# Per-head sums of squares of queries and keys: one full-precision product replaced by two single-rate products on a high/low split

## The chip, the cores and the metric

The kernel runs on one core of a Trainium2 chip. The metric is the device time of one execution in microseconds (us). The core has TensorE (PE, products), VectorE (DVE), ScalarE (ACT), GpSimd (POOL) and SyncE (SP, whose queue issues nearly all DMAs). Every engine and the SP queue work through their own instructions in order.

## The reference, cut to what matters

One layer of a decoder trunk, for 2048 prompt tokens and 8 sample tokens of width 1024:

```python
h = rmsnorm(x)*(1+scale1)+shift1
u, q, k, v, a_pool, a_attn = split(h @ w_in)
q = rope(rmsnorm(q.reshape(..., N_HEADS, HEAD_DIM), q_norm_g), pos)
k = rope(rmsnorm(k.reshape(..., N_HEADS, HEAD_DIM), k_norm_g), pos)
x += g1*(sig(a_pool)*(PoolMix(u) @ w_pool_br) + sig(a_attn)*(DilatedAttn(q,k,v) @ w_attn_br)) @ w_out
x += g2*relu(h2 @ w_up)**2 @ w_down
```

12 heads of 64 stand in 3 groups of 4 (g = 2, 1, 0). `rmsnorm` of a query or key divides each head by the root of the mean of its 64 squares. That sum of squares is what the change is about. Queries and keys are also outputs (the key windows) and the operands of the attention.

## The kernel before, in words

**Products.** Activations lie transposed, channels on the partitions. Each dense product with a weight is made of three products at the single rate on operands split into a high and a low part of type float32r (`mm3`, which calls `mm`, L153, for every product): high by high, high by low, low by high. A weight block (`load_w`, L178 to L186) comes by an SP DMA into a raw tile `wr` (3 buffers), ACT casts the high part (L183), POOL subtracts for the low part (L184), the pair being the tile `wh` (3 buffers). One block is loaded ahead.

**Stages.** Tokens go in two chunks. In the first one (1032 tokens, in pieces of 512, 256 and 264 columns) the projections for queries, keys and values run nearly alone, about 80 to 291 us. In the second chunk (1024 tokens, pieces of 512) they run from 742 to 1130 us, laced with the attention of groups that are ready (scores `ps_s`, transposes `ps_t`, outputs `ps_o`). After that come the gates, the output projection and the feed-forward products, which take most of the 3 ms.

**One query or key piece.** `qk_out` empties the two product tiles of a piece with ACT: a scaled copy `ab` (L381) and the squares `qsq` (L382). `after_qk` (L390 to L446) then runs 30 times: 18 with 512 columns (6 of them in the first chunk), 6 with 256 and 6 with 264. Each time it loads the rotary table `cs` (L395, SP), POOL adds the two square tiles (L396), POOL and DVE make the rotation (tiles `rt` and `ro`, L400 to L405), PE multiplies the added squares by a block of ones, which sums over the 32 partitions of each head and leaves the sum on all of them (`ps_hs`, a product in float32), ACT takes the root (L410), DVE the reciprocal (L411) and the two scalings (L413), ACT and POOL split the result into high and low (`ohl`, L423 and L424), and SP stores it to `qst` or `kst` (L426, L429) and for late keys to an output (L433). Later SP loads the attention's `slab` tiles from `qst` and `kst`. In the second chunk there is one `cs`, one `ohl`, two `qsq` and two product tiles in PSUM.

**What sets the order.** PE's order is written by hand: `Order` keeps an emulated clock which every product advances by a given duration, and the body of `after_qk` is a coroutine that comes back `HS_AT` (6500 ns of that clock) after it began, at the next poll, to put its `ps_hs` between other products. Attention batches are coroutines of the same kind. The other engines' order is made by a scheduler; instructions under `first()` get a higher priority.

**Start.** `opening` (first products while the conditioning is worked out) takes its raw weight tiles from the same 3 `wr` buffers. Constants, the block of ones `hones` among them, come in one DMA, the tile `cp` (L226).

## Time and profile before

| | before |
|---|---|
| runs, median (lowest to highest) of 3 | 3072.97 us (3070.19 to 3075.37) |
| the profiled execution, its own time | 3068.15 us |
| its span in the trace | 3066.3 us |
| mean granted clock of TensorE | 0.982 |
| busy: PE, DVE, ACT, POOL | 96%, 52%, 32%, 31% |
| PE products of `ps_hs` | 30 instructions, 60 records in the trace (two passes each) |

In a profile, the busy time of an engine is what its instructions took; the time an engine sat idle is put down to whatever ended the wait. A product's record covers more than its own step, since products are pipelined: its cost is read from the chain of waits, which follows PE from start to start.

### The profile page before, as it was taken

The page shows a single profiled execution, that of the slowest core. Times are in us where ns is not written, and L with a number is a line of the kernel's source. Part 1 is how long each engine was busy: PE and PEld are TensorE (multiplying, and loading weights), DVE is VectorE, ACT ScalarE, POOL GpSimd, SP SyncE. Part 2 cuts the span into 40 slices and gives each one's busy share as a digit, 9 for nine tenths or more (in the row PEclk, how much of TensorE's full clock was granted, in tenths as well). Part 3 has the DMA queues.
Part 4 walks back from the last instruction along what each step waited for, and adds up shares of the span by engine and source line. Part 5 has one row for each costly group of instructions (what it writes and reads, how often), then busy time and mean ns, then how long its engine had stood idle before and what let it go on. Part 6 is the DMA issues. An engine that isn't in the chain of part 4 may idle for free.

```text
span 3066.3 us, 40880 instructions
## 1 busy us (share of the span) xinstructions
PE 2956.4 (96%) x16220; PEld 2526.4 (82%) x16220; DVE 1590.4 (52%) x2645; ACT 970.6 (32%) x1765; POOL 960.6 (31%) x504
## 2 busy tenths in 40 slices
PE   7999999999898799999999999999999999999999
PEld 3899788887787688887899999999877788888887
DVE  5656442542744524447865555545578554444444
ACT  4333332434544434433521221221235212111211
POOL 2565341433433311224531222122245312221221
PEclk9999999999899889999999999999999999999999
DMA  6544752335777878876221111111272211111111
GB/s 239 176 139 156 275 174 91 129 107 151 198 191 209 186 191 217 235 233 236 94 96 35 56 49 46 45 49 49 84 250 83 76 42 56 48 49 42 55 43 68
DMA packets 204431, 379.09 MB, mean 124 GB/s; under 512 B 43232, under 2 KB 99904, under 8 KB 203456
## 3 DMA queue, kind: packets, MB, share of 16 engines
q1 hardware_dynamic: 192720, 359.63, 38.2%
q10 hardware_dynamic: 11520, 16.85, 1.5%
q8 instruction: 128, 2.10, 0.3%
q14 instruction: 63, 0.52, 0.1%
HBM read 294.89 MB, written 81.75 MB: 123 GB/s over the span
## 4 chain that ended last, share of the span: by engine, by line
PE 77%; DMA 6%; DVE 5%; issue 3%; ACT 2%; POOL 2%; SPq 1%; DVEq 0%; ACTq 0%; POOLq 0%
PE ps_dn L153 22%; PE ps_up L153 22%; PE ps_g L153 9%; PE ps_qk L153 5%; PE ps_v L153 4%; PE ps_wo L153 4%; PE ps_u L153 3%; PE ps_s L153 2%; PE ps_o L153 1%; PE ps_pb L153 1%; POOL wh L184 1%; PE ps_ada L153 1%; PE ps_ab L153 1%; DMA t1d<-ta 1%; DMA cs<-in_rope 1%
## 5 line engine op out<-in xcount | busy, mean ns | idle before, releaser
L184 POOL TENSOR_TENSOR wh<-wr,wh 128x1024 fp32r<-128x1024 f32 (+1 forms) x274 | 650.1, 2380 | 1679.0 <-ACT wh L183 1607.5
L153 PE MATMUL ps_dn<-rt,wh 128*128 128x512 f32 (+2 forms) x3840 | 726.2, 350 | 6.4 <-POOL wh L184 3.3
L153 PEld LDWEIGHTS ps_dn<-rt,wh 128*128 128x128 f32 x3840 | 618.9, 188 | 109.2 <-POOL wh L184 4.2
L183 ACT CAST wh<-wr 128x1024 fp32r<-128x1024 f32 (+1 forms) x306 | 309.4, 1023 | 730.7 <-issue 562.3
L1274 DVE SCALAR_TENSOR_TENSOR xa<-ps_dn,mod,xa 128x512 f32<-128x512 f32 (+1 forms) x640 | 405.2, 641 | 202.8 <-PE ps_dn L153 201.0
L153 PE MATMUL ps_g<-h,wh 128*128 128x512 f32 (+2 forms) x1920 | 390.5, 355 | 0.4 <-POOL wh L184 0.4
L153 PE MATMUL ps_up<-hb,wh 128*128 128x264 f32 (+2 forms) x2304 | 371.5, 320 | 0.0
L153 PE MATMUL ps_up<-ha,wh 128*128 128x512 f32 x1536 | 365.7, 394 | 0.0
L153 PEld LDWEIGHTS ps_up<-hb,wh 128*128 128x128 f32 x2304 | 332.3, 188 | 36.0
L153 PEld LDWEIGHTS ps_g<-h,wh 128*128 128x128 f32 x1920 | 309.4, 191 | 48.4 <-POOL wh L184 0.9
L153 PEld LDWEIGHTS ps_up<-ha,wh 128*128 128x128 f32 x1536 | 287.1, 188 | 64.2 <-issue 0.5
L153 PE MATMUL ps_qk<-h,wh 128*128 128x512 f32 (+2 forms) x1440 | 301.1, 363 | 8.9 <-POOL h L318 6.5
L1258 DVE TENSOR_TENSOR r<-r 128x512 f32<-128x512 f32 (+2 forms) x160 | 99.3, 620 | 387.0 <-ACT r L1257 386.9
L153 PEld LDWEIGHTS ps_qk<-h,wh 128*128 128x128 f32 x1440 | 235.9, 194 | 50.8 <-POOL h L318 7.5
L1260 DVE TENSOR_TENSOR rt<-r,rt 128x512 fp32r<-128x512 f32 (+2 forms) x160 | 217.8, 1361 | 81.8 <-ACT rt L1259 81.7
L1257 ACT ACTIVATE r<-ps_up 128x512 f32<-128x512 f32 (+2 forms) x160 | 82.1, 513 | 415.0 <-PE ps_up L153 415.0
L153 PE MATMUL ps_v<-wh,h 128*128 128x256 f32 (+1 forms) x1224 | 169.3, 294 | 24.5 <-ACT wh L183 18.9
L153 PEld LDWEIGHTS ps_v<-wh,h 128*128 128x128 f32 (+1 forms) x1224 | 155.2, 192 | 30.2 <-ACT wh L183 19.3
L914 ACT ACTIVATE pe<-pe,ost 128x128 f32<-128x128 f32 (+1 forms) x192 | 87.1, 455 | 153.2 <-DVE ost L912 149.9
L912 DVE CUSTOM_DVE_ANT_0 pe<-ps_s,cp 128x128 f32<-128x128 f32 (+1 forms) x192 | 61.4, 358 | 129.7 <-PE ps_s L153 129.7
L1259 ACT CAST rt<-r 128x512 fp32r<-128x512 f32 (+2 forms) x160 | 85.8, 536 | 66.3 <-DVE r L1258 66.3
L153 PE MATMUL ps_pb<-py,wh 128*128 128x512 f32 (+2 forms) x480 | 95.5, 358 | 6.6 <-ACT py L555 3.7
(181 smaller groups left out, 2985.4 us busy)
## 6 DMA issues: line engine op xcount, KB each, us to landing
wr<-in_w_up SPq DMA_DIRECT2D x72, 512.0 KB
wr<-in_w_down SPq DMA_DIRECT2D x68, 512.0 KB
wr<-in_w_in SPq DMA_DIRECT2D x64, 512.0 KB
wr<-in_w_ada SPq DMA_DIRECT2D x48, 512.0 KB
slab<-kst SPq DMA_DIRECT2D x40, 512.0 KB
wr<-in_w_out SPq DMA_DIRECT2D x32, 512.0 KB
cs<-in_rope SPq DMA_DIRECT2D x18, 512.0 KB
qst<-ohl SPq DMA_DIRECT2D x9, 1024.0 KB
```

Source lines behind the costliest of these rows:

```text
L153: PE.matmul(ps, w, x, start=start, stop=stop)
L183: S.copy(out=wt[:, 0, :n], in_=raw[:, :n])
L184: eng.tensor_tensor(out=wt[:, 1, :n], in0=raw[:, :n], in1=wt[:, 0, :n].bitcast(F32), op=ALU.subtract)
L912: V.tensor_tensor_reduce(out=pe[:, off:off + nk], in0=ps[:, off:off + nk], in1=mask[:, mo:mo + nk], scale=-0.125, scalar=3.0e38, op0=ALU.a ...
L914: S.activation(out=pe[:, off:off + nk], in_=pe[:, off:off + nk], func=AF.Exp, scale=-1.0, bias=o[:, 64:65], accum_out=o[:, 65:66])
L1257: S.activation(out=r1[:, :l], in_=ps[:, :l], func=AF.Relu)
L1258: V.tensor_tensor(out=r1[:, :l], in0=r1[:, :l], in1=r1[:, :l], op=ALU.mult)
L1259: S.copy(out=rt[:, 0, a:a + l], in_=r1[:, :l])
L1260: V.tensor_tensor(out=rt[:, 1, a:a + l], in0=r1[:, :l], in1=rt[:, 0, a:a + l].bitcast(F32), op=ALU.subtract)
L1274: V.scalar_tensor_tensor(out=x[:, c0 + a:c0 + a + lp], in0=ps[:, :lp], scalar=mod[:, 40 + m, 0:1], in1=x[:, c0 + a:c0 + a + lp], op0=ALU.m ...
```

## The change

Four edits. The emulated due time `HS_AT` goes from 6500 to 7500. `hones` leaves the constants' tile and comes by a DMA of its own into a `wr` buffer during `opening`, from where ACT casts it into a float32r tile. In `after_qk`, after POOL's addition, ACT casts the added squares to a float32r tile (high) and DVE subtracts that from them (low); the two tiles are of a ring of two buffers, `th`, that the gates also use. The float32 product is replaced by two float32r products that add up in the same PSUM tile, and on the emulated clock n/0.6 ns become twice n/2.4 + 2.5 ns.

```diff
-HS_AT = 6500
+HS_AT = 7500
...
-CPACK = (("cT", (8, 9)), ("bada", (48,)), ("gn", (2, 8)), ("ident", (128,)), ("ones", (128,)), ("hones", (128,)),
+CPACK = (("cT", (8, 9)), ("bada", (48,)), ("gn", (2, 8)), ("ident", (128,)), ("ones", (128,)), 
...
-    cT, ident, ones, hones, mask = cv["cT"], cv["ident"], cv["ones"], cv["hones"], cv["mask"]
+    cT, ident, ones, mask = cv["cT"], cv["ident"], cv["ones"], cv["mask"]
...
+    hones = cst.tile([P, P], F32R, name="hones")
...
             G.tensor_tensor(out=sq[:, 0, :n], in0=sq[:, 0, :n], in1=sq[:, 1, :n], op=ALU.add)
+
+            m = 1 if n > 256 else 2
+            hl = [gtp.tile([P, m, 512 // m], F32R, tag="th", bufs=2, name="sqhl") for _ in range(2 // m)]
+            sh, sl = (hl[0][:, 0, :n], hl[-1][:, m - 1, :n])
+            with first():
+                S.copy(out=sh, in_=sq[:, 0, :n])
+                V.tensor_tensor(out=sl, in0=sq[:, 0, :n], in1=sh.bitcast(F32), op=ALU.subtract)
...
-            small(pst[:, :n], hones, sq[:, 0, :n], n / 0.6)
+            mm(pst[:, :n], hones, sh, True, False, max(107.0, n / 2.4 + 2.5))
+            mm(pst[:, :n], hones, sl, False, True, max(107.0, n / 2.4 + 2.5))
...
         raws[3] = ada_load(op, 3)
+        raw = rawp.tile([P, 1024], F32, tag="wr", name="wr")
+        SP.dma_start(out=raw[:, :P], in_=I["hones"])
+        S.copy(out=hones, in_=raw[:, :P])
```

The changed lines shift later line numbers: the addition is L397, the cast L403, the low part L404, POOL's `ohl` L433, the stores to `qst` and `kst` of groups 1 and 0 L438, attention's stores L970.

The other engines' order moves with it. At the start of the second chunk (first two query pieces of group 2), POOL before:

```order
L396 TENSOR_TENSOR qsq<-qsq 128x512
L400 TENSOR_TENSOR rt<-ab,cs 128x512
L402 TENSOR_TENSOR rt<-ab,cs 128x512
L184 TENSOR_TENSOR wh<-wr,wh 128x1024
L402 TENSOR_TENSOR rt<-ab,cs 128x512
L424 TENSOR_TENSOR ohl<-ro,ohl 128x512 x2
L400 TENSOR_TENSOR rt<-ab,cs 128x512
L396 TENSOR_TENSOR qsq<-qsq 128x512
L184 TENSOR_TENSOR wh<-wr,wh 128x1024
```

and now:

```order
L397 TENSOR_TENSOR qsq<-qsq 128x512
L408 TENSOR_TENSOR rt<-ab,cs 128x512
L410 TENSOR_TENSOR rt<-ab,cs 128x512
L184 TENSOR_TENSOR wh<-wr,wh 128x1024
L408 TENSOR_TENSOR rt<-ab,cs 128x512
L397 TENSOR_TENSOR qsq<-qsq 128x512
L410 TENSOR_TENSOR rt<-ab,cs 128x512
L184 TENSOR_TENSOR wh<-wr,wh 128x1024
L433 TENSOR_TENSOR ohl<-ro,ohl 128x512 x2
```

The low part of the first piece's result (`ohl`) now stands behind the second piece's addition and a weight block.

At the end of that stage, the SP queue around the first key store of group 0 (`kst_74`), the table `cs` of the second key piece and the weight block `w_v` for the values of group 0, before:

```order
L395 DMA cs<-in_rope 128x2x512
L958 DMA att_79<-ost 128x4x66 x4
L950 DMA vt<-vscr 128x8x256
L395 DMA cs<-in_rope 128x2x512
L429 DMA kst_74<-ohl 512x1x512
L180 DMA wr<-in_w_v 128x1024
```

and now:

```order
L970 DMA att_79<-ost 128x4x66 x2
L438 DMA kst_74<-ohl 512x1x512
L970 DMA att_79<-ost 128x4x66 x2
L962 DMA vt<-vscr 128x8x256
L396 DMA cs<-in_rope 128x2x512
L180 DMA wr<-in_w_v 128x1024
```

The key store stands ahead of the table now, and two attention stores, the load `vt` and the table lie between it and the weight block.

On POOL, the same two key pieces of group 0, before:

```order
L396 TENSOR_TENSOR qsq<-qsq 128x512
L396 TENSOR_TENSOR qsq<-qsq 128x512
L400 TENSOR_TENSOR rt<-ab,cs 128x512
L402 TENSOR_TENSOR rt<-ab,cs 128x512
```

and now:

```order
L397 TENSOR_TENSOR qsq<-qsq 128x512
L408 TENSOR_TENSOR rt<-ab,cs 128x512
L410 TENSOR_TENSOR rt<-ab,cs 128x512
L397 TENSOR_TENSOR qsq<-qsq 128x512
```

The rotation of the first key piece no longer stands behind the second piece's addition.

## Rows read from the trace of the kernel before

**Rows 1.** The profile's page, part 1: busy us, share of the span, instructions.

```profile
PE 2956.4 (96%) x16220; PEld 2526.4 (82%) x16220; DVE 1590.4 (52%) x2645; ACT 970.6 (32%) x1765; POOL 960.6 (31%) x504
```

**Rows 2.** Busy time by stretch (columns: stretch, length, each engine's busy us, granted clock, DMA).

```profile
142.00:217.00 75.00, 75.00 (x526) 68.83 (x524) 43.27 (x56) 26.07 (x52) 46.70 (x39) 1.00 0.54 176
742.00:854.00 112.00, 103.38 (x588) 90.32 (x587) 60.07 (x111) 54.25 (x120) 44.65 (x26) 0.92 0.78 201
854.00:970.00 116.00, 105.16 (x626) 92.49 (x625) 62.82 (x114) 56.69 (x119) 45.63 (x27) 0.97 0.74 197
970.00:1076.00 106.00, 84.86 (x426) 73.99 (x424) 46.28 (x109) 47.81 (x120) 38.35 (x24) 0.90 0.78 190
```

**Rows 3.** Chain of waits in the first chunk (start us, us, product).

```profile
160.62 0.86 PE ps_hs L153 x2
161.48 5.09 PE ps_qk L153 x39
166.57 0.43 PE ps_hs L153 x2
167.00 6.24 PE ps_qk L153 x27
```

**Rows 4.** Waits of PE, 80 to 291 us (total us, times, longest).

```profile
PE ps_qk L153 <- POOL h L318: 3.7, 1, 3.7
PE ps_hs L153 <- POOL qsq L396: 1.7, 1, 1.7
```

**Rows 5.** Groups by shape, 80 to 291 us (count, busy us, mean ns, idle before).

```profile
L423 ACT CAST ohl<-ro 128x256 fp32r<-128x256 f32 x24 | 8.6, 404 | 57.8 <-DMA kst<-ohl 31.1 <-DMA qst<-ohl 26.7
```

**Rows 6.** Timeline, first key piece of 512 columns in group 1 (start us, us).

```profile
182.46 1.73 POOL L396 TENSOR_TENSOR qsq<-qsq 128x512 f32<-128x512 f32 x1
...
184.66 0.68 DVE L404 TENSOR_TENSOR ro<-ro,rt 128x512 f32<-128x512 f32 x1
...
184.80 1.02 PE L153 MATMUL ps_hs<-qsq,cp 128*128 128x512 f32 x2
```

**Rows 7.** Timeline of the opening, ACT.

```profile
49.42 1.03 ACT L183 CAST wh<-wr 128x1024 fp32r<-128x1024 f32 x1
```

**Rows 8.** Waits of PE, 742 to 1130 us.

```profile
PE ps_v L153 <- ACT wh L183: 18.9, 2, 16.4
...
PE ps_t L172 <- ACT px L922: 3.2, 3, 2.0
PE ps_o L153 <- ACT px L922: 3.2, 2, 1.6
```

**Rows 9.** Timeline around the first key store of group 0.

```profile
1051.19 0.59 ACT L382 ACTIVATE qsq<-ps_qk 128x512 f32<-128x512 f32 x1
...
1051.85 1.29 POOL L396 TENSOR_TENSOR qsq<-qsq 128x512 f32<-128x512 f32 x1 [14.98 <-ACT qsq L382]
...
1053.24 1.70 DVE L401 TENSOR_TENSOR ro<-ab,cs 128x512 f32<-128x512 f32 x1
...
1058.48 1.18 ACT L423 CAST ohl<-ro 128x512 fp32r<-128x512 f32 x2 [3.74 <-issue]
...
1061.69 0.57 SPq L429 DMA_DIRECT2D kst<-ohl  x1
...
1062.30 0.62 SPq L180 DMA_DIRECT2D wr<-in_w_v  x1
...
1069.06 1.04 ACT L183 CAST wh<-wr 128x1024 fp32r<-128x1024 f32 x1 [9.40 <-DMA wr<-in_w_v]
...
1070.15 0.80 PE L153 MATMUL ps_v<-wh,h 128*128 128x256 f32 x2 [16.38 <-ACT wh L183]
```

**Rows 10.** Timeline around the first query store of group 2.

```profile
778.99 0.57 SPq L426 DMA_DIRECT2D qst<-ohl  x1
...
782.20 2.85 POOL L184 TENSOR_TENSOR wh<-wr,wh 128x1024 fp32r<-128x1024 f32 x1
...
797.92 0.62 PE L153 MATMUL ps_s<-slab 128*128 128x128 f32 x4
```

## The prediction

> **What bounds the kernel now.** I read the page first: PE is busy 96% of the span and every other engine about half of it or less [rows 1], so PE time that goes away counts, unless PE waits instead. Next the stretches, because the 30 products in question lie in two of them only. In the first chunk's projections PE is busy for the whole stretch, 75.00 of 75 us [rows 2]; in the second chunk's, which are laced with attention, it is busy 103.38 of 112, 105.16 of 116 and 84.86 of 106 us [rows 2], so some 40 us there are waits. The longest is one of 16.4 us for the weights of the values of group 0 [rows 8]. The chain of waits gives prices from start to start [rows 3], and the timelines show which piece of work a wait hangs on. 0.2% of the time, about 6.1 us, is what a measurement of this kernel can tell from no change. The sum below is made against the profiled execution, 3068.15 us; it lies 4.8 us under the median of the runs, 3072.97 us, so I carry the difference over to the median.
>
> **The product itself.** One float32 product of 512 columns takes 0.86 us of the chain, one of 256 columns 0.43 [rows 3]. Single-rate products of 512 columns take 6.24/27 = 0.231 us, of 264 columns 5.09/39 = 0.131 [rows 3]. Two of them are 0.46 and 0.26 us. The saving is 0.40 us for each of 18 pieces and 0.17 for each of 12: 4.5 us in the first chunk (6 x 0.40 + 12 x 0.17) and 4.8 us in the second (12 x 0.40). 9.3 us is all that the edit can save on PE, 0.3% of the time.
>
> **First chunk.** PE has no gap there to lose a saving in, except two waits [rows 4]. The first piece stands ahead of the 3.7 us wait for `h`, and its 0.40 us are lost in that. Against the rest stands a longer way to the product: ACT's cast and DVE's subtraction now lie between POOL's addition and PE. A cast of 512 columns takes 1.18/2 = 0.59 us [rows 9], of 256 columns 0.40 [rows 5]; a DVE instruction with two inputs of 512 columns 0.68 us when POOL is quiet [rows 6] and 1.70 beside POOL's work [rows 9]. So the sum arrives 1.3 to 2.3 us later, and the due time gives 1.0 us of it back. For most pieces PE waits for no addition before [rows 4]. The tight ones are the first key piece of group 1, 184.80 - (182.46 + 1.73) = 0.6 us [rows 6], its like in group 0, and the last piece of group 2, which already waits 1.7 us for the addition [rows 4]. With 1.0 us more they have 1.6, 1.6 and 1.0 us: 0 to 0.7 us are missing in the first two, about 0.3 in the third, to which comes what the queues add. I take 1.5 us for them together, between 0 and 4. First chunk: -4.5 + 0.4 + 1.5 = **-2.6 us**.
>
> **Second chunk.** PE saves 4.8 us; three things are weighed against it.
>
> *The key store of group 0.* The 16.4 us wait ends when `w_v` is cast at 1069.06; its load was issued at 1062.30, right behind a key store at 1061.69 which waited for that piece's rotation [rows 9]. The rotation stood on POOL behind the next piece's addition, which waited 14.98 us for ACT's squares [rows 9]. Now the rotation goes first, and the store hangs on something else: ACT casts the second half of the result behind the cast of the next piece's squares. That cast can start when the addition ends, 1051.85 + 1.29 = 1053.1; with 0.6 us for it, 0.6 for the half and about 1.3 for POOL's low part the store goes at some 1055.8. Two attention stores, a load and the rotary table follow before `w_v`, 0.6 to 0.7 us each as the issues here [rows 9]: about 1058.5, 3.8 us earlier. I take **-3.5 us**; the bounds are 0 (if an attention store ahead waits) and -6.
>
> *ACT standing still.* The cast stands in ACT's queue behind the squares and waits there for POOL's addition: at least 1.29 us for 512 columns and 0.59 for the cast itself [rows 9]. Over 12 pieces 12 x 1.3 = 16 us of stalls and 7 us of work. ACT is about half busy [rows 2], but attention goes through it in a chain, and PE waited 3.2 + 3.2 us for ACT's copies `px` already [rows 8]. Between nothing and the 16 us I take a quarter, **+4 us**, since the emulated order leaves other products ahead of most of these steps, and only two such rows have PE waiting.
>
> *Stores that come later.* In group 2 the low part of the first query result now stands behind the next addition and a weight block, which ended at 782.20 + 2.85 = 785.05 [rows 10]; with its own 3 us the store goes at about 788, 9 us after 778.99 [rows 10]. Loads for the next scores stand behind it on SP; those scores come at 797.92 [rows 10], so most of the delay is covered, as only some of the loads stand behind it. A similar swap lies in group 1. Bounds 0 and 9 us; I take **+3 us**, near the lower end because the scores come 10 us behind the late store.
>
> **Start.** `hones` takes the third raw buffer, so one weight load waits until an earlier block is split. ACT casts the late block only at 49.42 [rows 7], and a load takes 1069.06 - 1062.30 = 6.8 us from issue to cast [rows 9], so issuing it by 42 us costs nothing; the worst, were it not covered, is those 6.8 us. I take nothing. From the gates on, the order of the engines is as before, and I put nothing there.
>
> **Sum.** -2.6 - 4.8 - 3.5 + 4 + 3 = -3.9 us: 3064.3 us for the profiled execution, **3069 us** for the median.
>
> **A rule that speaks against it.** DVE's two-input instruction took 1.70 us in one place and 0.68 in another, and the slow one ran beside POOL [rows 6, 9]; POOL's addition took 1.73 us in one place and 1.29 in another [rows 6, 9]. The Trainium skill, "SBUF — State Buffer", section "SBUF: two separate sides", says that a DVE instruction with two SBUF inputs and a GpSimd instruction reading SBUF take a shared port pair as an exclusive lock, so that one blocks the other. By that rule every added subtraction costs POOL time too, where POOL runs. From the rows alone: 12 subtractions, each 1.0 us longer and POOL 0.4 longer, would be at most 12 x 1.4 = 17 us more on the way from the squares to the store, in the stage where that way ends in waits. I have used 1.70 for the bound of the first chunk; in the second this is part of the second rival below.
>
> **The rivals.** *All of the saving stays.* For it: the first chunk's PE has no gaps [rows 2], and the missing time in the tight pieces is short of a microsecond each. Against it: the second chunk's gaps. Then -4.1 - 4.8 - 3.5 = -12.4 us: 3060.6 us.
>
> *Slower: the way from the squares to the stores becomes the bound in the second chunk.* ACT and SP work in order, so a cast that waits for POOL holds attention's exponentials, and a store that waits for `ohl` holds the loads behind it. The place is group 2 and group 1 of the second chunk; the price is half of ACT's 16 us, the 9 us of the late store in full, and no gain at `w_v`: -2.6 - 4.8 + 8 + 9 = +9.6 us, 3082.6 us. It decides where the slabs behind the late store land after 797.92, that is, if the store goes later than some 790. For it: most of PE's waits there are for ACT, 18.9 + 3.2 + 3.2 us [rows 8]. Against it: the due time gives back 1 us, and 10 us of cover at the store.
>
> *The pair isn't cheaper than the float32 product.* If each of the two took 0.43 us, PE would save nothing and only the added work would remain, -3.5 + 4 + 3 + 1.5, about +5 us: 3078 us. Against it: all other products on this path have the same type and take 0.231 us [rows 3].
>
> **How the numbers follow.** Forecast 0.45, all of the saving 0.27, slower 0.23, not cheaper 0.05. The bounds of the forecast's own terms reach about 6 us to either side, 3063 to 3075. The range reaches to both other cases, 3059 to 3082 us. Faster by over 0.2%: nearly all of the second case and a quarter of the first, 0.37. Slower by over 0.2%: most of the third and a little of the first and last, 0.21. In between 0.42.
>
> **What would show it.** Right: `ps_hs` at about 0.46 us for a pair of 512 columns in the chain; PE's busy share of the first chunk unchanged, the stretch 2 to 4 us shorter; the wait for `w_v` at some 13 us; a few more microseconds of waits of PE on `px` and on slabs. Wrong: waits of PE for `sqhl` in the first chunk above 2 us a group; the wait for `w_v` unchanged or gone; a new long wait for a slab or a weight in groups 2 and 1; or a gain or loss behind 1300 us, where nothing of the change stands.

## The result, and the profile after

The changed kernel takes **3093.69 us** (median of 6 runs, 3090.80 to 3099.68); the kernel before, beside it, 3069.78 us (6 runs, 3067.28 to 3075.37). The ratio is 1.0080, 95% interval [1.0069, 1.0091]: 24 us slower, where I forecast 4 us faster, and above the top of the range, 3082 us. The profiled execution of the changed kernel took 3093.65 us with a span of 3091.9 us.

Part 1 of its page (busy us, share, instructions), to be held against [rows 1]:

```profile
PE 2955.8 (96%) x16220; PEld 2525.2 (82%) x16220; DVE 1617.6 (52%) x2675; ACT 984.8 (32%) x1796; POOL 963.3 (31%) x504
```

PE is busy for as long as before, although its work has become less. So the 24 us are not work of PE. ACT gained 14.2 us and DVE 27.2 us in a span of 3092 us; neither is a bound by its total. What grew is time in which PE waits, and time in which it runs at its lower clock. Busy time by stretch (columns as in [rows 2]):

```profile
142.00:217.00 75.00, 71.90 (x489) 66.27 (x487) 51.95 (x70) 26.68 (x54) 46.03 (x36) 0.95 0.50 163
742.00:854.00 112.00, 98.15 (x502) 84.41 (x501) 59.88 (x98) 55.81 (x116) 49.46 (x27) 0.94 0.69 187
854.00:970.00 116.00, 106.72 (x658) 96.57 (x657) 61.90 (x114) 57.46 (x121) 43.91 (x28) 0.96 0.74 193
970.00:1076.00 106.00, 91.91 (x521) 82.18 (x519) 47.68 (x122) 52.27 (x132) 33.83 (x21) 0.96 0.79 200
```

The first chunk's stretch was full before (75.00 of 75 us at a granted clock of 1.00). Now PE stands still for 3.1 us of it, and the mean granted clock is 0.95.

**Where the time went.** I compare when the same product starts in the two traces: the first product of the first chunk's gates (`ps_g`) marks the end of its projections, the first `ps_qk` behind 500 us the start of the second chunk, the first `ps_wo` behind 1300 us the end of its projections, attention, gates and branches.

| | first chunk's gates begin | second chunk begins | second output projection begins | end of span |
|---|---|---|---|---|
| before | 291.0 | 742.7 | 1389.7 | 3066.3 |
| changed | 304.0 | 757.9 | 1411.0 | 3091.9 |
| later by | 13.0 | 15.2 | 21.3 | 25.6 |

Half of the loss in these two executions arises up to the end of the first chunk's projections, 2.2 us in the rest of that chunk, 6.1 in the second, and 4.3 behind it. Of the 13.0 us of the first chunk some 3.8 stand ahead of 83 us, in the opening; they are no part of my theory (last section). Nor can the 4.3 us at the end be put down to the change: two kernels below that lose nothing (the new order alone, the ring alone) take 3069.0 - 1388.4 = 1680.6 and 3070.7 - 1390.5 = 1680.2 us for that stretch, the changed kernel 1680.9, and only the profiled execution of the kernel before 1676.6. So some 17.5 us of the 25.6 stand where the change acts.

**The first chunk in rows.** Waits of PE from 80 to 291 us (columns as in [rows 4]):

```profile
PE ps_hs L153 <- DVE sqhl L404: 8.8, 4, 3.0
```

One of the four waits for the low part is the first key piece of group 1, the place of [rows 6]. Its timeline (start us, us; in brackets the idle time before it and what ended it):

```profile
188.16 1.76 POOL L397 TENSOR_TENSOR qsq<-qsq 128x512 f32<-128x512 f32 x1
...
189.95 0.62 ACT L403 CAST sqhl<-qsq 128x512 fp32r<-128x512 f32 x1 [3.10 <-POOL qsq L397]
190.47 0.68 DVE L411 TENSOR_TENSOR ro<-ab,cs 128x512 f32<-128x512 f32 x1
...
190.62 0.49 PE L153 MATMUL ps_hs<-sqhl,hones 128*128 128x512 f32 x1
...
191.07 1.21 DVE L412 TENSOR_TENSOR ro<-ro,rt 128x512 f32<-128x512 f32 x1
...
192.21 1.21 DVE L413 TENSOR_TENSOR ro<-ro,rt 128x512 f32<-128x512 f32 x1
193.33 0.68 DVE L404 TENSOR_TENSOR sqhl<-qsq,sqhl 128x512 fp32r<-128x512 f32 x1
...
194.07 0.80 PE L153 MATMUL ps_hs<-sqhl,hones 128*128 128x512 f32 x1 [2.96 <-DVE sqhl L404]
...
194.66 5.74 PE L153 MATMUL ps_qk<-h,wh 128*128 128x264 f32 x27
```

The addition ends at 189.92, the cast at 190.57, and PE does the product of the high part. The subtraction could start then; it starts at 193.33, because DVE works in order and three instructions of the same piece's rotation stand ahead of it. ACT itself stood idle for 3.10 us before the cast: the cast was its next instruction, and the addition was not done. The last row shows a second price. The 27 products behind the wait take (200.24 - 194.66)/27 = 0.207 us each until the next product at 200.24; before, the same form took 0.131 [rows 3]. The granted clock of 180 to 200 us, before and changed:

```profile
180.00:200.00 20.00, 20.00 (x162) 19.35 (x162) 15.22 (x15) 9.21 (x20) 17.49 (x16) 1.00 0.41 126
```

```profile
180.00:200.00 20.00, 16.90 (x107) 15.87 (x106) 14.00 (x16) 6.89 (x16) 11.49 (x11) 0.83 0.40 133
```

At 1.00 all of the stretch is at 2.4 GHz, at 0.83 about a third of it is at 1.2. The wait cost 3 us, and the products at the lower clock after it about 27 x (0.207 - 0.131) = 2 us more (an estimate from these rows).

**The second chunk in rows.** Waits of PE from 742 to 1130 us, to be held against [rows 8]:

```profile
PE ps_v L153 <- ACT wh L183: 23.5, 2, 17.7
PE ps_o L153 <- ACT px L934: 9.4, 3, 5.3
PE ps_t L172 <- ACT px L934: 5.4, 2, 2.9
```

The wait for `w_v` is 17.7 us, not the forecast 13, and attention's copies `px` cost PE 14.8 us instead of 6.4. Timeline of the changed kernel around the key store of group 0, the place of [rows 9] (ACT, then SP's queue):

```profile
1064.43 0.59 ACT L383 ACTIVATE qsq<-ps_qk 128x512 f32<-128x512 f32 x1
1064.91 0.62 ACT L432 CAST ohl<-ro 128x512 fp32r<-128x512 f32 x1
1066.41 0.62 ACT L403 CAST sqhl<-qsq 128x512 fp32r<-128x512 f32 x1 [0.88 <-POOL qsq L397]
1066.94 0.61 ACT L432 CAST ohl<-ro 128x512 fp32r<-128x512 f32 x1
1082.74 1.04 ACT L183 CAST wh<-wr 128x1024 fp32r<-128x1024 f32 x1 [15.19 <-DMA wr<-in_w_v]
```

```profile
1069.30 0.56 SPq L438 DMA_DIRECT2D kst<-ohl  x1
1069.95 1.72 SPq L970 DMA_DIRECT2D att<-ost  x2
1071.77 1.30 SPq L962 DMA_DIRECT2D vt<-vscr  x1
1073.12 1.03 SPq L396 DMA_DIRECT2D cs<-in_rope  x1
1074.21 0.60 SPq L180 DMA_DIRECT2D wr<-in_w_v  x1
```

The chain is the one that I described: the second half of the result (`ohl`, 1066.94) stands behind the next piece's cast, which waits for POOL, so the first key piece's store still hangs on the second piece's squares. From those squares to the issue of `w_v` it was 1062.30 - 1051.19 = 11.1 us [rows 9] and is 1074.21 - 1064.43 = 9.8: 1.3 us won instead of 3.8, since the rows between the store and the weight took longer. The load then took 1082.74 - 1074.21 = 8.5 us to the cast instead of 6.8, and the gain was gone.

### The profile page after: what moved, and what is told of

Read it like the earlier page. It is cut to its first block, busy times and chain, and to the rows that moved or that the text cites. A ratio compares the mean times of both kernels' runs of the same rounds, so it can differ in the third digit from the quotient of the medians.

```text
span 3091.9 us, 40927 instructions
## 1 busy us (share of the span) xinstructions
PE 2955.8 (96%) x16220; PEld 2525.2 (82%) x16220; DVE 1617.6 (52%) x2675; ACT 984.8 (32%) x1796; POOL 963.3 (31%) x504
## 4 chain that ended last, share of the span: by engine, by line
PE 59%; DVE 4%; DMA 3%; issue 3%; POOL 3%; ACT 2%; SPq 1%; POOLq 0%; DVEq 0%; ACTq 0%
PE ps_dn L153 23%; PE ps_up L153 22%; PE ps_g L153 4%; PE ps_wo L153 2%; PE ps_qk L153 2%; PE ps_s L153 2%; PE ps_o L153 2%; POOL wh L184 1%; PE ps_v L153 1%; DMA slab<-kst 1%; PE ps_t L172 1%; DMA cs<-in_rope 1%; DMA wr<-in_w_out 1%; PE ps_ab L153 0%; DVE t L1168 0%
```

## The experiments

Two theories. **The split:** the cast and the subtraction stand in the in-order queues of ACT and DVE and make everything behind them late. **The order:** on the emulated clock the pair is cheaper than the float32 product, and the due time is later, so PE's steps come in another order, and that order fits the other engines worse. Ratios are to runs of the kernel before on the same chip.

**The due time alone.** The kernel before, with

```diff
-HS_AT = 6500
+HS_AT = 7500
```

> The kernel before with one edit: the due time of the head sums is 7500 instead of 6500; product, constants and everything else as before. Theory A (the 24 us come from the low part arriving late, that is from the added cast and subtraction): the waits of PE for the sum stay at 1.7 us or less in the first chunk, the stretch 80 to 291 us stays within 2 us, the total within 6 us of before, about 3070 us. Theory B (the 24 us come from the moved order of the products, which the later due time sets): 10 us or more of the loss is here, 3080 to 3095 us, above all behind 1126 us.

Measured: 3071.85 us against 3070.69, ratio 1.0004 [0.9994, 1.0015]. The due time by itself costs nothing.

**Without the low part.** The changed kernel, with both products of the high part (a piece of 512 columns then takes one tile of the ring, not two):

```diff
-            hl = [gtp.tile([P, m, 512 // m], F32R, tag="th", bufs=2, name="sqhl") for _ in range(2 // m)]
+            hl = [gtp.tile([P, m, 512 // m], F32R, tag="th", bufs=2, name="sqhl") for _ in range(1)]
...
-                V.tensor_tensor(out=sl, in0=sq[:, 0, :n], in1=sh.bitcast(F32), op=ALU.subtract)
...
-            mm(pst[:, :n], hones, sl, False, True, max(107.0, n / 2.4 + 2.5))
+            mm(pst[:, :n], hones, sh, False, True, max(107.0, n / 2.4 + 2.5))
```

> The changed kernel without DVE's subtraction: both products read the high part, so the low part of the sums of squares is left out; PE's work is the same as in the changed kernel. Theory A (late low part): PE's waits for the split, 10.6 us in five places in the changed kernel, go to under 1 us, the first chunk (80 to 291 us) gets 9 us shorter or more, since the clock doesn't fall behind the waits either; total 3078 to 3086 us. Theory B (order): the total stays within 5 us of 3093.7 us.

Measured: 3089.26 us, 1.0064 [1.0049, 1.0079]. From 80 to 300 us PE's waits for `sqhl` fall to 0.4 us. But at most some 5 us of the 24 came back, and even those are not clear of the noise (the changed kernel's interval is [1.0069, 1.0091]). Other waits took their place: in that stretch PE now waits for weights, whose casts go through ACT's queue as the split's do:

```profile
PE ps_v L153 <- ACT wh L183: 3.9, 2, 2.0
PE ps_v L153 <- POOL wh L184: 3.6, 2, 1.9
```

**More time for the way.** The changed kernel with `HS_AT = 10500`.

> The changed kernel with the due time of the head sums at 10500 instead of 7500, so that the products stand 3 us later between the others. Theory A (late low part): the waits of PE for the split go from 10.6 us to under 2 us, the first chunk gets 6 to 9 us shorter; the second chunk may lose some of it, since stores and loads behind the sums come later; total 3080 to 3092 us. Theory B (the order by the due time is what costs): slower still, 3095 us or more.

Measured: 3094.93 us, 1.0085 [1.0069, 1.0100]. That is above the 3080 to 3092 us of a late low part. A product that comes 3 us later on the emulated clock does not help: what is late is not that product's operand alone.

**The block of ones by another buffer.** The changed kernel, its block of ones loaded by way of the gates' ring instead of a raw buffer:

```diff
-        raw = rawp.tile([P, 1024], F32, tag="wr", name="wr")
+        raw = gtp.tile([P, 512], F32, tag="th", bufs=2, name="th")
```

> The changed kernel with one edit: the block of ones is loaded through a buffer of the gates' ring instead of the third raw weight buffer, so that the third weight load needn't wait; the order on PE, DVE and POOL is the same row by row. If the raw buffer is what made the opening 4.9 us longer: the products at 85 us come within 1 us of before and the total falls by 4 to 5 us, to about 3089 us. If the opening's loss is the clock (granted clock 0.66 at 46 to 56 us) and no wait for a load: no change of the total beyond 2 us, and the third load's earlier issue shows in the trace without effect.

Measured: 3098.72 us, 1.0086 [1.0065, 1.0107]. The raw buffer costs nothing that shows: in the trace the first chunk's gates begin at 304.0 us, as in the changed kernel. The median lies 5 us above the changed kernel's, outside the 2 us of the expectation, but its four runs are 3087.12 and 3098.33 to 3099.61 us, so a median of four runs can be off by a few us here. That `hones` comes by a DMA and a cast of its own was tested in no run by itself.

**Where the split stands.** Four variants of the changed kernel: cast and subtraction without the higher priority (`with first()` left out), both on POOL (`G.tensor_copy`, `G.tensor_tensor`), both on DVE (`V.tensor_copy`), and both put into the queues 3.5 us of the emulated clock later:

```diff
+            yield 3500
+            with first():
+                S.copy(out=sh, in_=sq[:, 0, :n])
+                V.tensor_tensor(out=sl, in0=sq[:, 0, :n], in1=sh.bitcast(F32), op=ALU.subtract)
-            yield HS_AT
+            yield HS_AT - 3500
```

(the last with `HS_AT = 8500`, and without the lines at their old place).

> The changed kernel with the cast and the subtraction taken out of the higher priority, so that the scheduler places them where they fall. Theory C (ACT stands still in front of the cast until POOL's addition is done, 60.4 us in 28 places in the changed kernel, and what is queued behind it comes late): ACT's waits for POOL's addition shrink to a third or less, and the loss with them, 3075 to 3085 us, unless the split itself then comes late at PE, which would show as waits of PE for it. Theory A (the low part is late): the split comes later still, PE waits for it more than the 10.6 us of the changed kernel, total 3095 us or more.

> The changed kernel with both steps of the split on POOL, right behind the addition in POOL's own queue; ACT and DVE get nothing of the change. Theory C: ACT's waits for the addition are gone, PE's waits on ACT return to those of before; POOL gets some 2.6 us more for each of 18 pieces and 1.4 for each of 12, about 64 us, of which its gaps take most in the second chunk. 3070 to 3085 us. If POOL's time is what counts in the first chunk (it is busy for 60% of it), the first chunk stays as long as in the changed kernel or longer, and weights come late at PE.

> The changed kernel with both steps of the split on DVE. Theory C in its narrow form (it is ACT's place in the queue that costs): ACT's waits for the addition are gone and the total falls to 3070 to 3085 us. In its wide form (any engine that stands in order in front of POOL's addition pays): DVE shows the same waits for the addition, some 20 us or more, the rotation and the value copies behind it come late, and the total stays within 6 us of 3093.7 us.

> The changed kernel with the cast and the subtraction recorded 3.5 us of the emulated clock after the addition, so that they stand further back in ACT's and DVE's queues, and with the due time at 8500. Theory C: ACT's waits for the addition fall from 60 us to under 25 us, PE's waits fall with them, total 3072 to 3085 us. If any added step in these queues costs as much wherever it stands: within 5 us of 3093.7 us.

Measured: 3092.06 us, 1.0063 [1.0044, 1.0083]; 3104.25 us, 1.0102 [1.0081, 1.0124]; 3095.79 us, 1.0074 [1.0049, 1.0098]; 3091.22 us, 1.0074 [1.0057, 1.0090]. With the split on POOL or on DVE, ACT no longer stands in front of the split's cast (on DVE it is DVE that waits for the addition, 60.9 us in 14 places), and that does not help, so a stall of ACT alone is not the cause. POOL has the highest median, but its interval overlaps with the changed kernel's. Without the priority and with the later place ACT still waits 41.5 and 43.9 us for the addition, instead of 60.4; the expectations wanted a third and under 25 us. So these two edits took away too little of the stall to decide about it. None of the four comes near the kernel before.

**The split alone.** The kernel before with cast and subtraction added, whose results nobody reads; PE's order and its float32 product are those of before:

```diff
+            m = 1 if n > 256 else 2
+            hl = [gtp.tile([P, m, 512 // m], F32R, tag="th", bufs=2, name="sqhl") for _ in range(2 // m)]
+            sh, sl = (hl[0][:, 0, :n], hl[-1][:, m - 1, :n])
+            with first():
+                S.copy(out=sh, in_=sq[:, 0, :n])
+                V.tensor_tensor(out=sl, in0=sq[:, 0, :n], in1=sh.bitcast(F32), op=ALU.subtract)
```

> The split's work without PE's saving: the kernel before, with ACT's cast and DVE's subtraction added at the changed kernel's place and priority; nothing reads their result, the product stays the float32 one and PE's order is that of before row by row. Theory C: PE waits on ACT and weights come late as in the changed kernel, and without the 9.3 us saved the total is as in the changed kernel or longer, 3088 to 3105 us. Theory A (only PE's own wait for the low part costs): no loss, 3070 to 3076 us.

Measured: 3082.55 us against 3069.04, 1.0045 [1.0030, 1.0060]. Work that nobody reads costs 13.5 us, between the 3088 to 3105 us expected of the queues and the 3070 to 3076 of a late low part alone. ACT's waits from 80 to 1130 us show the stalls, before the cast of every piece:

```profile
ACT sqhl L401 <- POOL qsq L396: 68.5, 30, 4.6
```

In the changed kernel the same row reads

```profile
ACT sqhl L403 <- POOL qsq L397: 60.4, 28, 4.8
```

This settles half of the first theory: the split costs about 13 us even when no product waits for it and PE's order is that of before. Whether ACT's stalls, DVE's queue or something else about the two added operations makes it, this run does not separate.

**The order given back.** The changed kernel, with the emulated price and due time of before, so that PE's order is that of before row by row:

```diff
-HS_AT = 7500
+HS_AT = 6500
...
-            mm(pst[:, :n], hones, sh, True, False, max(107.0, n / 2.4 + 2.5))
-            mm(pst[:, :n], hones, sl, False, True, max(107.0, n / 2.4 + 2.5))
+            mm(pst[:, :n], hones, sh, True, False, n / 1.2)
+            mm(pst[:, :n], hones, sl, False, True, n / 1.2)
```

> The changed kernel with the emulated clock told the old price of the head sum (n/0.6 ns for the pair) and the old due time: PE's order is that of before row by row, with a pair in place of each float32 product; the split stands as in the changed kernel. Theory E (two separate losses: the split's work in ACT's and DVE's queues, some 13 us, and the order that the cheaper emulated price makes in the second chunk and behind it, some 10 to 20 us; the 9.3 us saved on PE are there): 3070 to 3080 us, the stretch from 742 us to the output projection within 3 us of before. If the split alone makes the whole loss: 3088 us or more.

Measured: 3080.20 us against 3071.09, 1.0027 [1.0017, 1.0037]. About 15 of the 24 us come back without an operation being taken away.

**The order alone.** The counterpart: the kernel before with the change's due time and price, so that PE's order is that of the changed kernel row by row:

```diff
-            small(pst[:, :n], hones, sq[:, 0, :n], n / 0.6)
+            small(pst[:, :n], hones, sq[:, 0, :n], 2 * max(107.0, n / 2.4 + 2.5))
```

> The kernel before, with the change's emulated price and due time for its float32 product: PE's order is that of the changed kernel row by row, while the product, the block of ones and the other engines' work are those of before. Theory (the order by itself costs some 13 us): about 3083 us, a ratio of 1.003 to 1.006, with the loss in the second chunk and the gates, and PE waits on `ps_g` and `ps_ab` for weights behind 1130 us as in the changed kernel. Rival (the order costs only together with a shorter way on PE or with the split): 3069 to 3073 us.

Measured: 3070.80 us (12 runs) against 3069.70 (29 runs), 1.0001 [0.9989, 1.0013]. The rival held: with the product of before the new order costs nothing. So the second theory falls in the form I had given it. The order makes no loss by itself; it costs only together with other edits. The trace shows one thing more. Waits of PE, 742 to 1130 us and 1130 to 1420 us, and for the second stretch those of before:

```profile
PE ps_v L153 <- ACT wh L183: 3.0, 1, 3.0
```

```profile
PE ps_g L153 <- POOL wh L184: 5.1, 4, 1.7
PE ps_g L153 <- ACT wh L183: 3.8, 2, 2.4
PE ps_ab L153 <- POOL wh L184: 3.3, 3, 2.2
...
PE ps_ab L153 <- ACT wh L183: 2.5, 2, 2.0
```

```profile
PE ps_ab L153 <- POOL wh L184: 3.0, 2, 2.4
...
PE ps_ab L153 <- ACT wh L183: 1.3, 2, 0.7
PE ps_g L153 <- POOL wh L184: 0.4, 1, 0.4
```

The 16.4 us wait for `w_v` [rows 8] is gone, and the last `ps_v` starts at 1108.0 us instead of 1125.4. But the next output projection starts at 1388.4 instead of 1389.7: gates and branches wait 14.7 us for their weights, where it was 4.7. Of the 17 us by which this kernel is ahead at the last `ps_v`, 1.3 are left at the output projection and none in its time. That wait, from which I took 3.5 us, is worth next to nothing at the end.

**One chunk at a time.** The changed kernel with price and due time of before in one chunk only, first in the second (`ci == 1`), then in the first (`ci == 0`):

```diff
-            yield HS_AT
+            yield (6500 if ci == 1 else HS_AT)
...
-            mm(pst[:, :n], hones, sh, True, False, max(107.0, n / 2.4 + 2.5))
+            mm(pst[:, :n], hones, sh, True, False, n / 1.2 if ci == 1 else max(107.0, n / 2.4 + 2.5))
```

(the product of the low part likewise).

> The changed kernel with the emulated price and due time of before in the second chunk alone: PE's order of the second chunk and the gates is that of before, that of the first chunk is the change's. If the order loses its time in the second chunk: about 3080 us, ratio near 1.003, as with the order of before everywhere. If it loses it in the first chunk: about 3093 us, ratio near 1.008.

> The counterpart: the changed kernel with the emulated price and due time of before in the first chunk alone. If the order loses its time in the second chunk: about 3093 us, ratio near 1.008. If in the first chunk: about 3080 us, ratio near 1.003.

Measured: 3082.73 us, 1.0037 [1.0024, 1.0050], and 3089.41 us, 1.0062 [1.0041, 1.0083]. Most of what the order costs in company of the other edits, it costs in the second chunk (11 of about 15 us). The 4 us that the first chunk's order seems to cost are not clear of the noise, as the interval overlaps with that of the changed kernel.

**No split at all.** POOL writes the sum in float32r at once, and one product takes it; the sums keep their high part only. Three versions: with the price of one single-rate product and due at 6500, with the price of before (PE's order then that of before row by row), and that with the due time 7500.

```diff
-            G.tensor_tensor(out=sq[:, 0, :n], in0=sq[:, 0, :n], in1=sq[:, 1, :n], op=ALU.add)
+            sh = gtp.tile([P, 512], F32R, tag="th", bufs=2, name="sqh")[:, :n]
+            G.tensor_tensor(out=sh, in0=sq[:, 0, :n], in1=sq[:, 1, :n], op=ALU.add)
...
+            mm(pst[:, :n], hones, sh, True, True, n / 0.6)
```

> PE's saving without the split's work: POOL's addition writes the sum as float32r, and one single-rate product reads it; the low part of the sums of squares is left out, ACT and DVE get nothing, the due time is 6500 as before; the block of ones comes as in the changed kernel. PE saves 0.63 us for each of 18 pieces and about 0.3 for each of 12, some 15 us. Theory C (the split's steps in the other engines' queues cost, not the products): the first chunk gets shorter by 4 to 7 us against before, the total 3055 to 3066 us. Theory D (the stage has no slack in the weights, and a faster PE only meets them sooner): the first chunk stays as long as before, waits of PE for weights take what was saved, total 3066 to 3075 us.

> The run with the high part alone (the low part left out, no cast, no subtraction), with the emulated clock told the old price, so that PE's order is that of before row by row and one single-rate product stands where the float32 one stood. PE's work is some 15 us less. Theory E: neither of the two losses is left, and a good part of the saving shows: 3054 to 3064 us. If a saving on PE in these stages is worth nothing, since the other engines set their pace: 3066 to 3073 us. If the shared ring of two buffers or the way the ones are loaded costs: 3075 us or more.

> One product of the sums as POOL writes them in float32r, no split (so the sums keep only the high part), with the emulated price of before and the due time 7500 instead of 6500. With the due time of before PE waited 6.1 us for two of POOL's additions in the opening stretch. If those waits and the slower clock behind them are what eats the saving: 3060 to 3067 us, under the kernel before. If the saving is eaten by the other engines' pace wherever it stands: 3069 to 3080 us.

Measured: 3093.06 us, 1.0068 [1.0042, 1.0094]; 3080.11 us, 1.0027 [1.0015, 1.0039]; 3078.90 us, 1.0027 [1.0013, 1.0040]. The split is gone, PE has up to 18 x (0.86 - 0.23) + 12 x (0.43 - 0.13) = 15 us less to do, by the prices of [rows 3], and the kernel is slower than before. The cheaper price, and with it another order, costs 13 us here too, without any split. That version has long waits behind the projections, from 1130 to 1420 us (the like of before stands above):

```profile
PE ps_g L153 <- ACT wh L183: 11.9, 4, 6.7
PE ps_g L153 <- POOL wh L184: 7.8, 4, 3.7
PE ps_ab L153 <- ACT wh L183: 5.2, 2, 4.6
```

The third, in its profiled execution, brings the first chunk's projections to their end at 288.4 us, 2.6 ahead of before, so some of the saving does arrive there; then the second chunk takes 655.4 us from its start to the output projection, against 647.0. The profile of the second version can't show its loss: that execution took 3069.80 us, the fastest of its ten, with a median of 3080.11.

**The long product back, without the split.** The second of these versions, with its product issued four times over, each writing the same result, which takes PE about as long as the float32 product:

```diff
-            mm(pst[:, :n], hones, sh, True, True, n / 0.6)
+            for _ in range(4):
+                mm(pst[:, :n], hones, sh, True, True, n / 2.4)
```

and, to exclude the ring, the kernel before with POOL's sum in a tile of the ring `th`, in float32 (`out=sh` as above, the float32 product reading it).

> As the kernel with the high part alone and PE's order of before, but its product is issued four times over, each writing the same result, so that a piece of 512 columns takes PE about 4 x 0.23 = 0.92 us, as the float32 product did. Everything else is the same. If the shorter product is what is given back (PE comes earlier to data that is not there and stands still): about 3070 us, ratio 1.000. If something else in that kernel costs the time (the tiles of the ring `th`, the block of ones by way of a raw buffer): 3085 to 3095 us, as four products undo the saving on top.

> The kernel before with one edit: POOL writes the added squares into a tile of the gates' ring `th`, in float32, and the float32 product reads them there. Order, product, price and due time are those of before. If the ring makes POOL wait for a tile that PE has not read yet, and this is what the kernel with the high part alone lost: 3078 to 3082 us, ratio near 1.003. If the ring costs nothing: 3069 to 3072 us.

Measured: 3075.53 us against 3071.06, 1.0016 [1.0005, 1.0027], and 3070.42 us, 0.9996 [0.9983, 1.0008]. The ring costs nothing (with the float32 sum in it). Three more products in each of 30 places, some 17 us of work for PE, did not make the kernel slower; it comes out 4.6 us faster than with one, though the intervals overlap. The expectation had 3070 us if the shorter product alone is what loses, so that is not all of it. Busy time from 742 to 1130 us, with one product and with four:

```profile
742.00:1130.00 388.00, 340.44 (x1962) 306.88 (x1961) 188.10 (x408) 181.29 (x428) 135.06 (x79) 0.91 0.76 193
```

```profile
742.00:1130.00 388.00, 347.73 (x2002) 312.37 (x2001) 186.09 (x408) 181.57 (x430) 137.21 (x80) 0.93 0.78 193
```

PE is busy for 7 us more with the longer product, at a higher clock, and the stage is no longer for it: from the second chunk's first product to the output projection it takes 645.0 us with four products and 646.6 with one. The added work went into waits. Two that the one product has and the four have not, or hardly (with one, then with four):

```profile
PE ps_t L172 <- ACT pe L920: 7.4, 3, 4.3
...
PE ps_qk L153 <- ACT wh L183: 3.9, 1, 3.9
```

```profile
PE ps_t L172 <- ACT pe L921: 1.3, 2, 1.2
```

Over all runs the mean granted clock of the span is 0.977 to 0.980 with one product (10 runs), 0.980 to 0.984 with four (12 runs). What lies between the two is PE's product alone. So a shorter product is no gain in the second chunk: PE comes earlier to data that others bring, waits longer, and is granted less clock. That it makes the kernel slower than the long one is not shown.

## Why the prediction was wrong

**The product itself: right.** In the changed trace the pairs of the first chunk take PE 167.22 - 166.75 = 0.47 us for 512 columns and 172.82 - 172.58 = 0.24 for 256:

```profile
166.75 0.63 PE L153 MATMUL ps_hs<-sqhl,hones 128*128 128x512 f32 x2
167.22 5.52 PE L153 MATMUL ps_qk<-h,wh 128*128 128x264 f32 x36
172.58 0.40 PE L153 MATMUL ps_hs<-sqhl,hones 128*128 128x256 f32 x2
172.82 6.41 PE L153 MATMUL ps_qk<-h,wh 128*128 128x512 f32 x27
```

I had 0.46 and 0.26, so the 9.3 us are right as PE's work. As a gain in time they are not: split and pair with the order of before cost 9.1 us, the unread split 13.5, so by the medians the pair was worth about 4.4 us of its 9.3 (the two intervals overlap); in the versions without a split nothing of the saving is left in the time. **The step that failed first is "PE time that goes away counts, unless PE waits instead"**: I booked the 9.3 us as won and set single waits against them. What the runs show in its place is that PE waited instead at many points, and that two things cost more than the pair saves: the split's two operations, 13.5 us unread, where I had 1.5 + 4, and the new order, which costs nothing with the long product and about 15 us together with the rest of the change, where I had priced single moves of it at -3.5 + 3.

**First chunk, -2.6 us: wrong.** It is 9 us longer (13.0 less the 3.8 of the opening). The failed step here is the 1.5 us, between 0 and 4, for the tight pieces. I named the right pieces, and priced the longer way as the two operations' durations, 1.3 to 2.3 us. In the first key piece of group 1 it was 4.1 us from the addition's end (189.92) to the subtraction's (194.01), of which 2.8 stood behind the rotation on DVE; of "what the queues add" I had put next to nothing into my 1.5 us. The waits of PE for `sqhl` are 8.8 us over three groups, my own sign of "wrong"; to them comes the lower clock, as in the rows above. And with the low part left out, other waits took their place: the queues were late, not one operand.

**Second chunk: near in sum by luck, not by its terms.** From its first product to its last `ps_v` it was 1125.4 - 742.7 = 382.7 us and is 1139.5 - 757.9 = 381.6; -1.1, where -4.8 - 3.5 + 4 + 3 gave -1.3. But the two stretches don't hold the same work: in the new order 20 of attention's products, some 2 us at 0.11 us each, come behind the last `ps_v`. And the terms are off: `w_v` gave nothing, by the rows above, and `px` cost 8.4 us more, where I had 4 for ACT standing still. ACT waits for POOL's addition in 28 of 30 pieces, 2.2 us each; I had 1.3. The first query store went 43.1 us after the chunk's start (800.99 - 757.9) instead of 36.3 (778.99 - 742.7), 6.8 later where I had 9, but PE's waits for slabs are 4.7 us against 4.0, so my 3 us for late stores were too much. Against the kernel with the same order and the float32 product (1108.0 - 745.8 = 362.2 us) the stretch is 19.4 us longer.

**"From the gates on, the order of the engines is as before, and I put nothing there": wrong.** From the last `ps_v` to the next output projection it was 264.3 us and is 271.5, some 2 of it the moved products; the 4.3 us behind that are not the change's, as said above. I had looked for moved instructions from the gates on, not for what arrives later. The whole stretch from the second chunk's first product to the output projection, with the same work in it, is the better measure. It was 647.0 us; with the split, the pair and the order of before in this chunk it is 647.0, in an execution that was the slowest of its twelve; with the new order and the float32 product 642.6; with the new order and the rest of the change 653.1, that is 6.1 us more than before, where my terms gave 1.3 less. That the new order makes this loss only together with the other edits is shown; which moved batch, or which late data, makes it is not.

**The rivals.** The slower one had ACT in order behind POOL and a place in groups 2 and 1 of the second chunk. ACT's stalls are there, 60.4 us in all, and DVE's queue does the same; the late store cost little. The loss stands in large part in the first chunk, where I had excluded it for want of gaps. That PE has no gap means that nothing there covers a delay. The rival in which all of the saving stays falls with the version without a split. The pair that isn't cheaper falls by the rows above.

**The rule on the shared port** (the Trainium skill, "SBUF — State Buffer", section "SBUF: two separate sides") was weighed as up to 17 us. The trace agrees with it on DVE's side. Of the 30 subtractions ten began while a POOL instruction was running, and took 1.09 to 2.66 us; the other twenty took 0.42 to 0.69. One of the ten, of 264 columns, begins 0.51 us into POOL's work on a weight block and ends 0.28 us behind it:

```profile
253.56 2.41 POOL L184 TENSOR_TENSOR wh<-wr,wh 128x1024 fp32r<-128x1024 f32 x1
254.07 2.18 DVE L404 TENSOR_TENSOR sqhl<-qsq,sqhl 128x264 fp32r<-128x264 f32 x1 [1.09 <-ACT sqhl L403]
```

All 30 of them (least, median and longest in ns, then first and last start), and the twelve of the second chunk by themselves (count, busy us, mean ns):

```profile
L404 DVE TENSOR_TENSOR sqhl<-qsq,sqhl x30: 416/680/2659, 88.8 to 1067.1; 128x512 fp32r<-128x512 f32 x18, 128x256 fp32r<-128x256 f32 x6, 128x264 fp32r<-128x264 f32 x6
```

```profile
L404 DVE TENSOR_TENSOR sqhl<-qsq,sqhl 128x512 fp32r<-128x512 f32 x12 | 15.4, 1284 | 51.5 <-ACT sqhl L403 51.3
```

So in the second chunk the price is 15.4 - 12 x 0.68 = 7 us on DVE, where I had bounded it at 12. On POOL, where I had 0.4 us a piece, none shows: the additions have a median of 1.28 us in the changed kernel and 1.29 before.

```profile
L397 POOL TENSOR_TENSOR qsq<-qsq x30: 727/1280/1758, 86.9 to 1065.1; 128x512 f32<-128x512 f32 x18, 128x256 f32<-128x256 f32 x6, 128x264 f32<-128x264 f32 x6
```

How much of this reaches the time of the kernel no run here separates.

**What stays open.** About 4.5 us of the version with four products, against before, have no cause that I have shown. It differs from the kernel before in the product, in POOL's output type, and in the block of ones with its own DMA and cast; the last two were not tested alone. Nor is it shown what in the split makes its 13.5 us. No version here beats the kernel before.

## What to carry to other kernels

Price an operation that you add to an in-order queue by what stands ahead of and behind it there, not by its duration: 30 casts and 30 subtractions, most of them of 0.4 to 0.7 us, cost 13.5 us here without anybody reading them. Ask of an engine that looks full whether the engines that feed it can keep pace with a shorter instruction; test that by giving back the work without the edit, as the four-fold product does. A long wait is worth what is left of it at the next point that all the work must pass: a 16 us wait vanished in one kernel, and the time stayed the same.

## What the runs showed of the hardware

The granted clock fell where PE had stood still (0.83 instead of 1.00 from 180 to 200 us, around a wait of 2.96 us), and over whole runs it is lower in the kernels that lose. Averaged over the runs it is 0.9823 before (29 runs) and 0.9829 with the new order alone, 0.9798 with the unread split, 0.9793 with split and order of before, 0.9788 in the changed kernel, 0.9783 with the high part alone. The last is the version with the order of before. As the two levels are 1.2 and 2.4 GHz, span times one minus the clock is an upper estimate of the time given up to the lower level, upper because it counts waits too: 3067.9 x 0.0177 = 54 us before, 3078.3 x 0.0217 = 67 us with the high part alone. The difference, 12 us, is of the size of that kernel's loss of 9. It does not say which of the two, the waits or the clock, comes first.

The opening, up to 80 us, ran at 0.87 in the profiled execution of the changed kernel and at 0.91 in that of before. The kernel with the unread split, whose opening is written as before, has 0.87 too, and the high part alone with the order of before, whose opening is the change's, 0.91. So up to 4 us of one profile's time there are not to be read as the change's.
